# First norm's modulation as two fused VectorE instructions, with another order of the recurrent units and later booked transfer landings

## The chip, the cores and the metric

The kernel runs on one core of one Trainium2 chip. The metric is the device time of one launch in microseconds (us). In this text PE is TensorE, DVE is VectorE, ACT is ScalarE, POOL is GpSimd and SP is the engine that issues most transfers.

## The reference

One inference step of a two-layer decoder trunk: 512 prompt rows of width 1024, and 8 samples of 8 rows each, all in fp32. Layer 0 is a recurrent block (a causal convolution of width 4, sigmoid gates, a linear recurrence, a gelu branch), layer 1 sliding-window attention; each is followed by a gated feed-forward block of inner width 2816. Every norm is modulated by a shift and a scale that a vector of conditions gives, so the first steps are:

```
def rms_norm(x, g):
    y = xf * lax.rsqrt(jnp.mean(xf * xf, axis=-1, keepdims=True) + EPS)
    return (y * g.astype(jnp.float32)).astype(x.dtype)

sh1, sc1, g1, sh2, sc2, g2 = ada_mod(c, ada_w[l], ada_b[l], 6)   # silu(c) @ ada_w + ada_b
h = modulate(rms_norm(x, norm_g[l, 0]), sh1, sc1)                # h * (1 + scale) + shift
xr, yg = jnp.split(h @ w_in, 2, axis=-1)                         # recurrent block
...
x = x + g1[:, None, :] * out
h = modulate(rms_norm(x, norm_g[l, 1]), sh2, sc2)
x = x + g2[:, None, :] * swiglu(h, ffn_w_in[l], ffn_w_out[l])
```

Between the layers one shared projection makes keys and values from the stream. The outputs are the normed stream, the last convolution rows and recurrent states, and the key and value windows.

## The kernel before

**Number format and tiles.** The stream x lies in SBUF with its 1024 features as 8 chunks of 128 partitions and its rows along the free dimension, in two halves A and B of 288 columns (256 prompt columns, HP, and 32 of samples). A product of fp32 accuracy is made from three matmuls in the rounded format fp32r: each operand is split into a high part hi (the value rounded) and a low part lo (the value less hi), and PE adds hi by hi, hi by lo and lo by hi. So one output block of 128 features and one half is 8 chunks x 3 = 24 matmuls of 128x288. Weights come by DMA into four slots `raw`; ACT makes their high part (CAST `wh<-raw`), DVE their low part (TENSOR_TENSOR `wh<-raw,wh`), which also frees the raw slot. Modulated activations are the tiles `h` (one for each half, hi and lo side by side); gates read `ta` (hi) and `tb` (lo).

**The first norm.** `modulated` (line 911 of before) does chunk by chunk x times the inverse root (`rstd`, which the trace calls `acc`), then times scale plus shift (`mods`), then the split. The string M1 names engines: the first product by DVE, but by POOL for chunks 2 and 5; the value v by one DVE TENSOR_SCALAR into a `tb` slot; hi by ACT directly from the first product with scale and bias; lo = v - hi by DVE. The sample columns have their own function. The modulation comes from PE in four groups of two chunks (`ada_first`): PE's columns go to PSUM (`ada`), ACT copies them (`td`), PE transposes them back (`ada<-ident,td`) and DVE adds bias and norm weight (`mods`). The weights of all this, `ada_w` and `rnn_w_in`, come in a fixed order of transfers from SP.

**The order of work.** The kernel's functions do not issue instructions: a recorder collects every operation, which is why all of them carry line 505, and `schedule` (line 240) writes the order for each of the five engines once, with a cost model. Engines then run that order strictly, each instruction waiting for its operands' semaphores. The model's guess when a transfer has landed decides what it sets before what. It keeps one clock for the DMA engines, which starts at OFF (line 70), and books a landing at the end of a transfer's turn plus a margin (line 406):

```
b = max(s + op.cost + 650, dma_free[0])
dma_free[0] = b + op.lat
op.end = b + op.lat + (1700 if op.i >= self.strict else 1000)
```

The first transfers, up to `strict` (line 2029), have the smaller margin. A tile from a pool gets a slot when the schedule finds one free, so the order also decides which transfer waits for whom: 4 `raw` slots, 10 of `wh`, 37 of `sl`, 7 of `ta`, 8 of `tb`, 4 of `td`.

The recurrent block's own sequence is the string RNN (line 59): x0 to x7 are blocks of the convolution branch (16 or 24 matmuls a half), g0 to g7 the gates of a block (matmuls of 128x300 on `ta`, `tb`), y0 to y7 the gelu branch's blocks, which are multiplied by the recurrence's result and split into `sl` tiles. Half B follows half A by some units. ACT holds one table of functions at a time; exp, sqrt, gelu and silu are in separate tables (the gates use tanh, exp and sqrt, the y blocks gelu), and each change is an ACT_TABLE_LOAD.

`x_turn` (line 639) transposes the rows of x through PE at the start, `x_half` (line 1987) sums their squares. PE runs filler matmuls on the identity (`mm<-ident`) while it has no work.

Of the kernel before, what the change touches and what calls it, by code (L numbers as in the profile page):

```python
# [12 lines left out]
F32 = mybir.dt.float32  # L13
# [3 lines left out]
ALU = mybir.AluOpType  # L17
# [38 lines left out]
QUAD = (3, 4, 5, 6)  # L56
QK = 2
YT = lambda td, ta, sl: td
RNN = "x0 x1 x2 x3 x4 x5 g0 g1 g2 y2 y0 y1 g3 g4 x6 y3 x7 g5 y5 g6 y6 g7 y4 y7"
ATT = "q0A q2A a0A q1A q0B a2A q1B q3A a0B q2B q4A a1A a1B a4A a3A q3B a2B q5A q4B a3B q6A a5A q5B q7A a6A a4B s0A a5B s1A s2A s3A q6B q7B a7A s0B s1B a6B fA a7B o0A s2B s3B o1A o2A fB"  # L60
LOOK = {"PE": 24, "DVE": 24, "ACT": 24, "POOL": 24, "SP": 24}
NRAW = 4
# [2 lines left out]
XB = 100  # L65
NFILL = 60
AE = 100
ME = 30
YG = 6
OFF = 2300.0  # L70
AF_ = (1, 2, 4, 4)
NSL, NTA, NTB, NTD = 37, 7, 8, 4

# [70 lines left out]
class Recorder:  # L144
# [95 lines left out]
    def schedule(self):  # L240
# [64 lines left out]
        while n_left:  # L305
# [92 lines left out]
            if op.lat:  # L398

                free[e] = s + op.cost  # L400
                if e == "POOL":
                    op.end = s + op.cost + (3000 if op.i < self.strict else 5000)
                else:
                    b = max(s + op.cost + 650, dma_free[0])
                    dma_free[0] = b + op.lat
                    op.end = b + op.lat + (1700 if op.i >= self.strict else 1000)
            else:
                op.end = free[e] = s + cost
            for n in op.tiles:
# [122 lines left out]
def trunk_kernel(ctx, tc, a):  # L532
# [106 lines left out]
    def x_turn(t):  # L639
        src = xt[t].f  # L640
        if t < 4:
            for q in range(2):
                pt = aux()
                for k in range(4):
                    c = 4 * q + k
                    T.transpose(pt[:, k * P : (k + 1) * P], src[:, c * P : (c + 1) * P], ident[:])
                dst = x[t // 2][:, 4 * q : 4 * q + 4, (t % 2) * P : (t % 2) * P + P]
                (V.tensor_copy, S.copy)[q](dst, pt.rearrange("p (k n) -> p k n", k=4))
        else:
            pt = aux()  # L650
            for c in range(4):
                T.transpose(pt[:, c * P : (c + 1) * P], src[:, c * P : (c + 1) * P], ident[:])
            for h in range(2):
                V.tensor_copy(x[h][:, :, HP:HC].rearrange("p (q c) n -> p q c n", q=2), pt.rearrange("p (c q n) -> p q c n", c=4, q=2)[:, :, :, 32 * h : 32 * h + 32])
        xt[t].done()
# [255 lines left out]
    def modulated(h, gsc, gsh, how, cs=slice(0, KC), xn=None, known=False):  # L911

        batch, se, ne, ve, le = how.split()
        pick = {"V": V, "G": G}
        for c in range(cs.start, cs.stop):
            if (c - cs.start) % int(batch) == 0:
                modulated_samples(h, gsc, gsh, pick[se], slice(c, min(c + int(batch), cs.stop)), xn, known)
            t, u = xn[c] if xn else ta(), tb()
            n, v = t.f[:, 0:HP], u.f[:, 0:HP]
            hi, lo = [h4r(h)[:, c, i, 0:HP] for i in range(2)]  # L920
            if not known:
                pick[ne[c % len(ne)]].tensor_tensor(n, x[h][:, c, 0:HP], rstd[h][:, 0:HP], ALU.mult)
            w = ve[c % len(ve)]
            if w == "S":
                S.activation(v, n, AF.Identity, bias=mp(gsh, c), scale=mp(gsc, c))
            else:
                V.tensor_scalar(v, n, mp(gsc, c), mp(gsh, c), ALU.mult, ALU.add)
            if w == "F":
                S.activation(hi, n, AF.Identity, bias=mp(gsh, c), scale=mp(gsc, c))
            else:  # L930
                S.copy(hi, v)
            pick[le[c % len(le)]].tensor_tensor(lo, v, hi.bitcast(F32), ALU.subtract)
            if not xn or known:
                t.done()
            u.done()
        if known:
            xn[KC].done()
# [85 lines left out]
    def h4r(h):  # L1023
        return H[h].r.rearrange("p (c s n) -> p c s n", c=KC, s=2)
# [962 lines left out]
    def x_half(h):  # L1987
        st = tst[h]
        for t in ((0, 1, 4), (2, 3))[h]:

            r = raws() if h else None
            w = r.f if h else x[1].rearrange("p c n -> p (c n)")[:, D * (t % 2) : D * (t % 2 + 1)]
            n, y = (512, tst[1][:, 2:3]) if t == 4 else (D, st[:, t % 2 : t % 2 + 1])
            src, dst = xt[t].f[:, 0:n], w[:, 0:n]
            if t % 2 == 0:
                S.activation(dst, src, AF.Square, accum_out=y)
            else:
                V.tensor_tensor_reduce(out=dst, in0=src, in1=src, op0=ALU.mult, op1=ALU.add, scale=1.0, scalar=0.0, accum_out=y)
            if h:
                r.done()  # L2000
            if t == 4:
                V.tensor_copy(tst[1][0:64, 5:6], y[64:128])
                V.tensor_tensor(y[0:64], y[0:64], tst[1][0:64, 5:6], ALU.add)
                V.tensor_scalar(tst[0][0:32, 2:3], y[0:32], 1.0 / D, EPS, ALU.mult, ALU.add)
                V.tensor_scalar(tst[1][32:64, 2:3], y[32:64], 1.0 / D, EPS, ALU.mult, ALU.add)
# [49 lines left out]

    stages.append(jobs)
    stages.append(ffn1)
    pace = [0.0]

    def do(j, h):  # L2060
        for u in j.need:
# [121 lines left out]
```

## Time and profile before

| what | before |
|---|---|
| three runs, us | 1246.37, 1246.6, 1246.83 (median 1246.6) |
| profiled execution, us | 1247.9 |
| its span (first to last record), us | 1246.1 |
| PE busy, us | 1232.9 |
| DVE, ACT, POOL busy, us | 897.3, 653.3, 465.4 |
| table loads of ACT | 21 of 1283 ns |

The profiled execution took 1.3 us more than the median of the runs, and 1.8 us of it lie outside its span. In the rows below, times in a timeline are microseconds from the start of the span; the number in brackets is how long the engine stood idle ahead of the row, and what ended that. Groups give busy time, then mean ns of one instruction; a group's mean duration is longer than the distance between two starts, as an engine's instructions overlap a little.

### The profile page before, as it was taken

How to read it: one execution, taken by the hardware profiler on the slowest of the kernel's cores; microseconds unless marked ns; L12 is line 12 of the kernel's file. 1: busy time of each engine (PE TensorE's matmuls, PEld its weight loads, DVE VectorE, ACT ScalarE, POOL GpSimd, SP SyncE). 2: the span in 40 equal slices, each digit the busy share in tenths (PEclk: the TensorE clock that was granted, in tenths of full speed). 3: DMA queues.
4: the chain of work that ended last, by engine and by line, in shares of the span. 5: the costliest groups of instructions: out<-in, count | busy, mean ns of one | idle time of the engine just before them, and what ended most of it. 6: DMA issues, size and time to landing. Idle time of an engine off the chain costs nothing.

```text
span 1246.1 us, 25373 instructions
## 1 busy us (share of the span) xinstructions
PE 1232.9 (99%) x9590; PEld 1171.4 (94%) x9590; DVE 897.3 (72%) x2137; ACT 653.3 (52%) x1461; POOL 465.4 (37%) x645
## 2 busy tenths in 40 slices
PE   8999999999999999999999999999999999999997
PEld 7888989999999999998999988999999999999997
DVE  6998875895674786477578888568767667747766
ACT  5678954852452444145367679448425435525533
POOL 3264540163441452246125445100436246335500
PEclk9999999999999999999999999999999999999999
DMA  9985554326556555445433321422332323323222
GB/s 310 300 274 173 179 167 139 124 76 212 170 189 200 170 171 165 165 142 155 118 90 69 70 61 46 122 71 100 99 103 69 112 76 102 102 85 86 85 86 76
DMA packets 221164, 165.39 MB, mean 133 GB/s; under 512 B 23817, under 2 KB 205993, under 8 KB 221010
## 3 DMA queue, kind: packets, MB, share of 16 engines
q1 hardware_dynamic: 220434, 163.39, 43.1%
q8 instruction: 75, 1.23, 0.4%
q0 software_dynamic: 608, 0.39, 0.1%
q14 instruction: 47, 0.39, 0.1%
HBM read 160.85 MB, written 4.87 MB: 133 GB/s over the span
## 4 chain that ended last, share of the span: by engine, by line
PE 92%; DVE 3%; DMA 2%; ACT 1%; POOL 1%; issue 0%; SPq 0%; DVEq 0%; ACTq 0%
PE mm L505 87%; PE ada L505 5%; DVE sl L505 1%; DVE ta L505 1%; DMA reg<-in_x_prompt_dram 1%; DMA raw<-in_rnn_w_in_dram 1%; DMA wh<-in_ada_w_dram 1%; DVE wh L505 0%; DMA raw<-in_ffn_w_out_dram 0%; POOL td L505 0%; DVE h L505 0%; DVE x L505 0%; ACT wh L505 0%; SPq L505 0%; DVE tb L505 0%
## 5 line engine op out<-in xcount | busy, mean ns | idle before, releaser
L505 PE MATMUL mm<-h,wh 128*128 128x288 f32 x4080 | 584.1, 297 | 0.3
L505 PEld LDWEIGHTS mm<-h,wh 128*128 128x128 f32 x4080 | 553.0, 188 | 12.1 <-issue 6.0
L505 PE MATMUL mm<-sl,wh 128*128 128x288 f32 x3237 | 464.2, 296 | 0.3 <-ACT sl L505 0.3
L505 PEld LDWEIGHTS mm<-sl,wh 128*128 128x128 f32 x3237 | 439.8, 188 | 6.1 <-issue 5.0
L505 ACT CAST wh<-raw 128x512 fp32r<-128x512 f32 (+3 forms) x394 | 270.5, 706 | 304.2 <-PE mm L505 188.2
L505 DVE TENSOR_TENSOR wh<-raw,wh 128x512 fp32r<-128x512 f32 (+3 forms) x396 | 362.1, 935 | 58.4 <-ACT wh L505 53.9
L505 POOL TENSOR_TENSOR raw<-raw 128x512 f32<-128x512 f32 x78 | 115.2, 1477 | 175.5 <-DVE wh L505 157.9
L505 DVE SCALAR_TENSOR_TENSOR x<-mm,mods,x 128x256 f32<-128x256 f32 x160 | 77.3, 483 | 124.6 <-PE mm L505 123.8
L505 POOL TENSOR_TENSOR x<-x,ta 128x32 f32<-128x32 f32 x120 | 41.6, 347 | 241.1 <-DVE ta L505 241.1
L505 POOL TENSOR_TENSOR raw<-raw,raw 128x512 f32<-128x512 f32 x78 | 116.1, 1488 | 4.6
L505 PE MATMUL mm<-tb,wh 128*128 128x288 f32 (+1 forms) x500 | 92.7, 299 | 1.3 <-DVE td L505 1.3
L505 POOL TENSOR_TENSOR td<-td,td 128x288 f32<-128x288 f32 x39 | 33.1, 850 | 135.8 <-ACT td L505 121.3
L505 PEld LDWEIGHTS mm<-tb,wh 128*128 128x128 f32 x500 | 74.5, 188 | 4.3 <-DVE td L505 2.9
L505 ACT ACTIVATE ta<-x 128x288 f32<-128x288 f32 (+1 forms) x56 | 24.4, 442 | 63.4 <-POOL x L505 40.4
L505 PE MATMUL mm<-ta,wh 128*128 128x288 f32 (+1 forms) x259 | 57.4, 297 | 0.0
L505 DVE TENSOR_TENSOR td<-mm,td 128x288 f32<-128x288 f32 x78 | 34.4, 452 | 21.6 <-PE mm L505 21.0
L505 DVE TENSOR_TENSOR sl<-td,sl 128x288 fp32r<-128x288 f32 x65 | 41.2, 637 | 8.9 <-ACT sl L505 8.9
L505 PE MATMUL ada<-reg,cz 128*32 128x512 f32 (+1 forms) x408 | 47.0, 547 | 0.0
L505 PEld LDWEIGHTS mm<-ta,wh 128*128 128x128 f32 x259 | 42.8, 188 | 1.0 <-ACT ta L505 1.0
L505 ACT ACTIVATE td<-td 128x288 f32<-128x288 f32 x39 | 17.3, 443 | 44.2 <-DVE td L505 44.2
L505 ACT ACTIVATE ta<-ta,stat 128x256 f32<-128x256 f32 (+2 forms) x72 | 32.5, 473 | 10.8 <-DVE stat L505 10.4
L505 ACT COPY ta<-mm 128x288 f32<-128x288 f32 (+1 forms) x51 | 19.1, 376 | 36.2 <-PE mm L505 35.1
(221 smaller groups left out, 1243.9 us busy)
## 6 DMA issues: line engine op xcount, KB each, us to landing
raw<-in_ffn_w_in_dram SPq DMA_DIRECT2D x88, 512.0 KB
reg<-in_ada_w_dram SPq DMA_DIRECT2D x72, 512.0 KB
raw<-in_ffn_w_out_dram SPq DMA_DIRECT2D x32, 384.0 KB
raw<-in_ffn_w_out_dram SPq DMA_DIRECT2D x32, 320.0 KB
reg<-in_kv_ada_w_dram SPq DMA_DIRECT2D x14, 512.0 KB
raw<-in_rnn_w_in_dram SPq DMA_DIRECT2D x13, 512.0 KB
wh<-in_ada_w_dram SPq DMA_DIRECT2D x24, 256.0 KB
raw<-in_rnn_w_out_dram SPq DMA_DIRECT2D x8, 512.0 KB
```

The lines of the kernel that those rows point to most:

```text
L505: self.rec.add(eng, lambda: getattr(obj, name)(*map(real, args), **{k: real(v) for k, v in kw.items()}), cost, outs, ins, func, lat, port, ...
```

## The change

In `modulated`, for chunks 2 to 7 (`c >= FU`) where no product is handed in, DVE makes n = (x * scale) * rstd in one SCALAR_TENSOR_TENSOR, ACT makes hi = n + shift rounded, and DVE makes lo = (n + shift) - hi in a second SCALAR_TENSOR_TENSOR. No `tb` slot and no POOL instruction is used for these 256 columns. The first product therefore reads `mods`, which it did not before. The sequence RNN is another one: g0 comes ahead of x5, y1 y2 y0 in place of y2 y0 y1, g5 y5 y3 x7 in place of y3 x7 g5 y5. OFF goes from 2300 to 1800, and the booked margins from 1000 and 1700 to 2000 and 2900. The new constants SQ, XE and A0 have the values that give the same instructions as before.

```diff
-RNN = "x0 x1 x2 x3 x4 x5 g0 g1 g2 y2 y0 y1 g3 g4 x6 y3 x7 g5 y5 g6 y6 g7 y4 y7"
+RNN = "x0 x1 x2 x3 x4 g0 x5 g1 g2 y1 y2 y0 g3 g4 x6 g5 y5 y3 x7 g6 y6 g7 y4 y7"
...
+A0 = 0.0
+FU = 2
+SQ = 3
+XE = "VSVS"
...
-OFF = 2300.0
+OFF = 1800.0
...
-                    op.end = b + op.lat + (1700 if op.i >= self.strict else 1000)
+                    op.end = b + op.lat + (2900 if op.i >= self.strict else 2000)
...
-                (V.tensor_copy, S.copy)[q](dst, pt.rearrange("p (k n) -> p k n", k=4))
+                (V.tensor_copy if XE[t // 2 * 2 + q] == "V" else S.copy)(dst, pt.rearrange("p (k n) -> p k n", k=4))
...
+            hi, lo = [h4r(h)[:, c, i, 0:HP] for i in range(2)]
+            if c >= FU and not xn:
+                t = ta()
+                n = t.f[:, 0:HP]
+                V.scalar_tensor_tensor(n, x[h][:, c, 0:HP], mp(gsc, c), rstd[h][:, 0:HP], ALU.mult, ALU.mult)
+                S.activation(hi, n, AF.Identity, bias=mp(gsh, c))
+                V.scalar_tensor_tensor(lo, n, mp(gsh, c), hi.bitcast(F32), ALU.add, ALU.subtract)
+                t.done()
+                continue
             t, u = xn[c] if xn else ta(), tb()
             n, v = t.f[:, 0:HP], u.f[:, 0:HP]
-            hi, lo = [h4r(h)[:, c, i, 0:HP] for i in range(2)]
...
-            if t % 2 == 0:
+            if t % 2 == 0 or t > SQ:
...
-    pace = [0.0]
+    pace = [A0]
```

The first place in the program is on DVE, the last group of the first norm (chunks 6 and 7; `h_485` is half B before, `h_483` after). Before, the rows from the group's modulation on are these:

```order
L505 SCALAR_TENSOR_TENSOR mods<-ada_835,abT,vecT 128x9 x2
L505 TENSOR_TENSOR mods<-ada_835,abT 128x18
L505 TENSOR_TENSOR tb_850<-ta_664,mods 128x64
L505 TENSOR_SCALAR tb_854<-ta_775,mods 128x256
L505 TENSOR_TENSOR tb_850<-tb_850,mods 128x64
L505 TENSOR_SCALAR tb_862<-ta_811,mods 128x256
L505 TENSOR_TENSOR tb_866<-ta_813,mods 128x64
L505 TENSOR_SCALAR tb_870<-ta_815,mods 128x256
L505 TENSOR_TENSOR h_328<-tb_850,h_328 128x2x32
L505 TENSOR_TENSOR h_328<-tb_854,h_328 128x256
L505 TENSOR_TENSOR h_328<-tb_862,h_328 128x256
L505 TENSOR_TENSOR tb_866<-tb_866,mods 128x64
```

After, the rows from the same modulation on are these:

```order
L509 SCALAR_TENSOR_TENSOR mods<-ada_823,abT,vecT 128x9 x2
L509 TENSOR_TENSOR mods<-ada_823,abT 128x18
L509 SCALAR_TENSOR_TENSOR ta_839<-x_64,mods,acc_69 128x256
L509 TENSOR_TENSOR tb_846<-ta_428,mods 128x64
L509 SCALAR_TENSOR_TENSOR ta_849<-x_64,mods,acc_69 128x256
L509 TENSOR_TENSOR tb_846<-tb_846,mods 128x64
L509 TENSOR_TENSOR tb_858<-ta_653,mods 128x64
L509 SCALAR_TENSOR_TENSOR h_330<-ta_839,mods,h_330 128x256
L509 TENSOR_TENSOR tb_858<-tb_858,mods 128x64
L509 SCALAR_TENSOR_TENSOR h_330<-ta_849,mods,h_330 128x256
L509 TENSOR_TENSOR h_330<-tb_846,h_330 128x2x32
L509 TENSOR_TENSOR h_483<-tb_858,h_483 128x2x32
```

The four first products of the group, which stood ahead of the modulation before (among them `ta_775`, `ta_811`), now stand behind it and read `mods`; two of them, and two low parts, follow the rows shown, with one weight's low part between.

The second place is on PE, where gate g0's first matmuls stand (`h_485` and `h_483` are half B; the gates read `ta` and `tb`). Before, they stand behind a block of half A:

```order
L505 MATMUL mm_1102<-h_328,wh_1027 128x288
L505 MATMUL mm_1139<-ta_973,wh_1001 128x300
L505 MATMUL mm_1139<-ta_973,wh_1088 128x300
L505 MATMUL mm_1139<-tb_1111,wh_1001 128x300
L505 MATMUL mm_1147<-ta_973,wh_1001 128x300
L505 MATMUL mm_1147<-ta_973,wh_1088 128x300
L505 MATMUL mm_1147<-tb_1111,wh_1001 128x300
L505 MATMUL mm_1154<-h_485,wh_833 128x288 x2
```

After, they stand behind a block of half B:

```order
L509 MATMUL mm_1054<-h_483,wh_672 128x288
L509 MATMUL mm_1108<-ta_990,wh_965 128x300
L509 MATMUL mm_1108<-ta_990,wh_1082 128x300
L509 MATMUL mm_1113<-ta_990,wh_965 128x300
L509 MATMUL mm_1113<-ta_990,wh_1082 128x300
L509 MATMUL mm_1116<-h_483,wh_820 128x288 x2
L509 MATMUL mm_1116<-h_483,wh_894 128x288
L509 MATMUL mm_1116<-h_483,wh_820 128x288
L509 MATMUL mm_1125<-h_330,wh_1110 128x288 x2
L509 MATMUL mm_1116<-h_483,wh_820 128x288
L509 MATMUL mm_1116<-h_483,wh_894 128x288
L509 MATMUL mm_1116<-h_483,wh_820 128x288 x2
```

Before, all six of the two gate products stand together behind 18 matmuls of the next block; now the four that read `ta` come first, right behind the block of 24, then ten matmuls of two other blocks, then the two that read `tb`.

The third place is on DVE, where the first unit of the feed-forward block's output weights is split (`wh` of 128x640 from `raw`; `td` holds silu of the gate, which this DVE instruction multiplies by the other half's product before it is split for PE). Before, the rows from the end of the input weights' splits on are these:

```order
L505 TENSOR_TENSOR wh_3960<-raw_3841,wh_3960 128x512
L505 TENSOR_TENSOR wh_4000<-raw_3778,wh_4000 128x512
L505 TENSOR_TENSOR wh_4029<-raw_3849,wh_3911 128x640
L505 TENSOR_TENSOR sl_4038<-td_3827,sl_4016 128x288
L505 TENSOR_TENSOR wh_4045<-raw_3857,wh_3926 128x640
L505 TENSOR_TENSOR sl_4055<-ta_3758,sl_3992 128x288
L505 TENSOR_TENSOR mm_4003<-mm_4003,ta_3938 128x288
L505 COPY td_4062<-mm_4003 128x288
L505 TENSOR_TENSOR td_4062<-mm_3984,td_4062 128x288
L505 TENSOR_TENSOR wh_4091<-raw_4023,wh_4078 128x640
L505 TENSOR_TENSOR td_4008<-mm_4003,td_4008 128x288
L505 TENSOR_TENSOR wh_4112<-raw_4032,wh_4095 128x640
```

After, the rows from the same splits on are these:

```order
L509 TENSOR_TENSOR wh_3960<-raw_3819,wh_3960 128x512
L509 TENSOR_TENSOR wh_3981<-raw_3756,wh_3981 128x512
L509 TENSOR_TENSOR wh_4005<-raw_3756,wh_4005 128x512
L509 TENSOR_TENSOR wh_4027<-raw_3835,wh_3921 128x640
L509 TENSOR_TENSOR sl_4036<-td_3805,sl_4022 128x288
L509 TENSOR_TENSOR sl_4043<-ta_3736,sl_3971 128x288
L509 TENSOR_TENSOR wh_4050<-raw_3929,wh_3994 128x640
L509 TENSOR_TENSOR mm_3996<-mm_3996,ta_3917 128x288
L509 COPY td_4062<-mm_3996 128x288
L509 TENSOR_TENSOR wh_4075<-raw_3990,wh_4058 128x640
L509 TENSOR_TENSOR td_4062<-mm_3962,td_4062 128x288
L509 TENSOR_TENSOR td_3988<-mm_3996,td_3988 128x288
```

Before, the split of the third load (`raw_4023`) stands between the two `td` rows that precede PE's products; after, the first load's split is already over (row `wh_3914<-raw_3827`, six rows ahead of those shown), and the splits of the third and the fourth (`raw_3929`, `raw_3990`) both stand ahead of both `td` rows.

## The prediction

> **What bounds the kernel now.** I read the page first, then the waits of TensorE (PE), then the windows of the first 180 us, then the places where PE stands still. The page:
>
> ```profile
> span 1246.1 us, 25373 instructions
> PE 1232.9 (99%) x9590; PEld 1171.4 (94%) x9590; DVE 897.3 (72%) x2137; ACT 653.3 (52%) x1461; POOL 465.4 (37%) x645
> PE 92%; DVE 3%; DMA 2%; ACT 1%; POOL 1%; issue 0%; SPq 0%; DVEq 0%; ACTq 0%
> ```
>
> PE is busy 1232.9 of 1246.1 us and makes up 92% of the chain that ended last. The change touches no matmul of the model, so it can only move what PE waits for. Those waits, by kind (us in total, times, longest):
>
> ```profile
> PE mm L505 <- DVE td L505: 1.3, 1, 1.3
> PE ada L505 <- ACT td L505: 1.0, 1, 1.0
> PE mm L505 <- ACT sl L505: 0.3, 1, 0.3
> ```
>
> Seen whole, there is little to win: 1.3 us on a VectorE (DVE) result, 1.0 on a ScalarE (ACT) result, 0.3 on another; the rest are waits of the very start and two of 0.2. Windows (first PE, PEld, DVE, ACT, POOL busy, then granted clock, DMA share, GB/s):
>
> ```profile
> 30.00:40.00 10.00, 8.96 (x113) 7.88 (x112) 8.29 (x30) 6.49 (x15) 1.11 (x2) 1.00 1.10 336
> 60.00:80.00 20.00, 20.00 (x153) 17.81 (x146) 17.56 (x41) 13.13 (x26) 13.42 (x38) 1.00 0.95 296
> 80.00:100.00 20.00, 19.98 (x151) 18.30 (x150) 17.47 (x31) 17.08 (x34) 10.29 (x23) 1.00 0.59 190
> 100.00:120.00 20.00, 20.00 (x154) 16.80 (x153) 16.16 (x33) 17.08 (x29) 8.35 (x19) 1.00 0.46 140
> 120.00:140.00 20.00, 20.00 (x150) 19.82 (x149) 18.45 (x34) 17.90 (x37) 10.56 (x18) 1.00 0.73 238
> 140.00:160.00 20.00, 20.00 (x154) 16.78 (x153) 17.76 (x32) 18.54 (x34) 13.00 (x30) 1.00 0.53 166
> ```
>
> Up to 40 us the sixteen DMA engines have no room (share 1.10): the first norm runs inside a stage that loads set. From 60 to 160 us, the recurrent block, PE is full, but ACT is busy 83.73 of 100 us (13.13 + 17.08 + 17.08 + 17.90 + 18.54) and DVE 87.40: that stage has the least spare room beside PE. The base of my sum is the profiled execution (1247.9 us, its span 1246.1); it lies 1.3 above the median of the runs, 1246.6, to which I apply the difference.
>
> **The change part by part.** *First norm, chunks 2 to 7, both halves: 12 chunk-halves.* Groups of DVE and of GpSimd (POOL) in the norm's stretch, busy us and mean ns:
>
> ```profile
> L505 DVE SCALAR_TENSOR_TENSOR sl<-td,vecT,sl 128x300 f32<-128x300 f32 x18 | 8.3, 518 | 0.0
> L505 DVE TENSOR_TENSOR h<-tb,h 128x256 fp32r<-128x256 f32 x16 | 6.6, 420 | 0.0
> L505 DVE TENSOR_SCALAR tb<-ta,mods 128x256 f32<-128x256 f32 x14 | 5.7, 407 | 0.0
> L505 DVE TENSOR_TENSOR ta<-x,acc 128x256 f32<-128x256 f32 x10 | 4.1, 417 | 0.0
> L505 POOL TENSOR_TENSOR ta<-x,acc 128x256 f32<-128x256 f32 x4 | 3.5, 875 | 16.8 <-ACT acc L505 10.5 <-DVE ta L505 5.4 <-DVE tb L505 0.9
> ```
>
> Before, a chunk-half costs DVE 417 + 407 + 420 = 1244 ns, or 827 where POOL makes the first product (chunks 2 and 5, four chunk-halves). After, it costs two SCALAR_TENSOR_TENSOR of 128x256. That form with this shape is not in the trace: the floor is the TENSOR_TENSOR of the same shape, 417, the ceiling the 128x300 form, 518; I take 470, nearer the middle since 300 columns are 17% more. So 8 x (940 - 1244) = -2.4 us and 4 x (940 - 827) = +0.5: DVE is relieved of 1.9 us (3.3 to 0.6 at the ends: 8 x -0.41 to -0.21, 4 x +0.01 to +0.21), POOL of 4 x 0.875 = 3.5. POOL is idle most of that time, and DVE's relief is worth something only where PE waits for DVE.
>
> The Trainium skill, Vector Engine (DVE) Microarchitecture Reference, section 7 (points that are easy to get wrong), says the contrary of a cheap fusion: a scalar-tensor-tensor with two SBUF sources that are not bf16 runs at half throughput. The 128x300 row above has just such sources and takes 518 ns, near the plain two-source rows; the trace does not show the halving. By the rule the two instructions would take longer than the three; that is a rival below.
>
> But the order matters more than the sum: before, the product x times root needed no modulation and filled DVE's idle time ahead of it; now it needs the scale, so it comes after. The last group, chunks 6 and 7 (DVE, then PE):
>
> ```profile
> 43.85 1.22 DVE L505 TENSOR_TENSOR ta<-x,acc 128x256 f32<-128x256 f32 x4
> 46.87 0.36 DVE L505 SCALAR_TENSOR_TENSOR mods<-ada,abT,vecT 128x9 f32<-128x9 f32 x2 [0.91 <-PE ada L505]
> 50.50 0.55 DVE L505 TENSOR_TENSOR h<-tb,h 128x64 fp32r<-128x64 f32 x2
> 50.97 0.95 DVE L505 TENSOR_TENSOR wh<-raw,wh 128x768 fp32r<-128x768 f32 x1
> ```
>
> ```profile
> 46.50 0.33 PE L505 MATMUL ada<-ident,td 128*128 128x128 f32 x1
> 46.59 12.21 PE L505 MATMUL mm<-h,wh 128*128 128x288 f32 x88
> ```
>
> Before, four products ran at 43.85, ahead of the modulation at 46.87, and the last piece of half B was there at 51.05. By the new order DVE does eight scalar-tensor-tensors and the small ones between 47.3 and the end, with the split of one weight (0.95) ahead of the last two: 8 x 0.40 (starts of such instructions in a row stand about 0.07 closer than their mean) + 8 small at 0.16 + 0.95 = 5.4, so 52.7 at worst and, as the last two are half B's last two chunks, chunk 6 at about 52.0. PE takes 12.21 / 88 = 0.139 per matmul; 37 of them stand ahead of chunk 6 of half B, so it is asked for at 46.59 + 5.1 = 51.7. That is a new wait of 0.3 us; bounds 0 and 1.0. **+0.3.**
>
> *Start.* In the new order PE transposes the bias vector before the eight of x, and it has one filler more.
>
> ```profile
> 5.45 1.04 PE L505 MATMUL mm<-ident,reg 128*128 128x128 f32 x8
> 7.17 0.23 PE L505 MATMUL mm<-ident,sl 16*128 16x16 f32 x1 [0.68 <-DMA sl<-in_ada_b_dram]
> ```
>
> The eight began at 5.45; after, they follow the vector's transposition, which ends at 7.40, so they begin 1.9 later, of which the wait of 0.68, now ahead of them, is given back. Behind them stands this pinch:
>
> ```profile
> 36.62 1.04 ACT L505 CAST wh<-raw 128x1024 fp32r<-128x1024 f32 x1 [2.77 <-DMA raw<-in_rnn_w_in_dram]
> 37.58 0.26 ACT L505 COPY td<-ada 128x128 f32<-128x128 f32 x1
> 37.89 0.33 PE L505 MATMUL ada<-ident,td 128*128 128x128 f32 x1 [1.04 <-ACT td L505]
> ```
>
> ACT copies what PE needs only behind a cast that waits for a weight until 36.62. The order of ACT there, and of the loads up to that weight, is the same after, so the pinch stays and swallows lateness up to 1.04 us ahead of it. **0** (0 to +1.2, which is 1.9 less 0.7, if that cover were gone).
>
> *Units' order, the booked start of the transfers, later booked landings.* They move the recurrent block's instructions. Gate g0 follows the 24 matmuls of one unit directly. Before:
>
> ```profile
> 60.58 5.88 PE L505 MATMUL mm<-h,wh 128*128 128x288 f32 x42
> 59.26 1.28 ACT L505 ACT_TABLE_LOAD   x1
> 64.27 0.47 DVE L505 TENSOR_TENSOR tb<-sl,ta 128x300 fp32r<-128x300 f32 x1
> 66.57 0.30 PE L505 MATMUL mm<-tb,wh 128*128 128x300 f32 x1
> ```
>
> Its low part is ready at 64.74 and used at 66.57; after, g0 stands behind the first 24 of the 42 matmuls, so it starts at 60.58 + 24 x 0.139 = 63.9, and the low part is asked for 14 matmuls later, at 65.85: of 1.8 us slack 1.1 stays, and the lateness of the norm's end (0.3 to 1.7) lies against it. I take +0.1, bounds 0 and 0.6. ACT's table loads go from 21 to 23, both extra ones in this stage: 2 x 1.28 = 2.6 us on an engine with 100 - 83.73 = 16.3 idle. Hidden on average; I charge +0.1 for places where they are not, bounds 0 and 2.6. **+0.2.**
>
> *End of the block.* PE's 0.3 wait:
>
> ```profile
> 174.35 0.43 ACT L505 CAST sl<-td 128x288 fp32r<-128x288 f32 x1 [0.93 <-DVE ta L505]
> 174.83 5.40 PE L505 MATMUL mm<-sl,wh 128*128 128x288 f32 x38 [0.25 <-ACT sl L505]
> ```
>
> The new order has one table load fewer in this tail and the last gate unit's matmuls earlier: **-0.3** (0 to -0.4).
>
> *First feed-forward block, at 284 us*, PE's longest wait (DMA from the chain, then ACT, DVE, PE):
>
> ```profile
> 278.74 5.09 DMA raw<-in_ffn_w_out_dram
> ```
>
> ```profile
> 275.90 3.72 DVE L505 TENSOR_TENSOR wh<-raw,wh 128x512 fp32r<-128x512 f32 x4
> 284.67 0.82 DVE L505 TENSOR_TENSOR wh<-raw,wh 128x640 fp32r<-128x640 f32 x1 [2.15 <-ACT wh L505]
> 285.41 0.45 DVE L505 TENSOR_TENSOR td<-mm,td 128x288 f32<-128x288 f32 x1
> ```
>
> ```profile
> 283.91 0.73 ACT L505 CAST wh<-raw 128x640 fp32r<-128x640 f32 x1 [3.22 <-DMA raw<-in_ffn_w_out_dram]
> 285.92 0.67 PE L505 MATMUL mm<-tb,wh 128*128 128x288 f32 x3 [1.27 <-DVE td L505]
> ```
>
> The third load of the out weights waits until a slot is freed by the third of the four splits (275.90 + 3 x 0.93 = 278.69); DVE's td stands behind that load's split. After, the first out weight is split ahead of the group, so the third load goes early; the fourth takes the slot, freed by the second split, one split (3.72 / 4 = 0.93) sooner. It lands at 278.74 - 0.93 + 5.09 = 282.9; cast 0.73, split 0.8, and now both td behind it, 0.4 each: 285.2 against 285.9, so the wait falls from 1.3 to 0.6. **-0.7** (-1.3 if it lands in time, +1.0 if the load goes no sooner and both td queue behind it).
>
> The rest, from 300 us on, is nearly the same order; 0, give or take 0.5. Sum: 0.3 + 0 + 0.2 - 0.3 - 0.7 = **-0.5**: 1247.4 for an execution like the profiled one, 1246.1 by the median.
>
> **The rivals.** *A, slower: the recurrent block becomes ACT's.* The two table loads (2.6) and the norm's late end (up to 1.7) fall where gates come sooner, and ACT, at 18.54 of 20 from 140 to 160, cannot give it back. PE then waits 4.3, less the 1.0 above: 1246.6 + 3.3 = 1249.9. It decides once g0's low part is over 1.1 us late and ACT's idle time from 60 to 160 falls under some 3 us. Against: 16.3 us idle now.
>
> *B, faster: every wait behind the start goes.* 1.04 at 37.9, 1.27 at 285.9, 0.25 at 174.8: -2.6, 1244.0, and somewhat less if the start shrinks with them. For: DVE and POOL are lighter up to 50 us. Against: the wait at 37.9 ends with a landing that the order of loads sets.
>
> *C, the fused form at half rate.* If the form with both sources in SBUF ran so, a 128x256 would take some 0.82 us, twice the plain 0.41. Eight of them in the last group end 8 x (0.82 - 0.47) = 2.8 later, and the wait at 51.7 grows by as much: 1246.1 + 2.8 = 1248.9. Against it: the 518 itself, a quarter over the plain form of 256. The rule for it is the one of the Trainium skill cited above.
>
> *D, nothing of it reaches PE*, as the stalls only swap places: 1246.6.
>
> **How the numbers follow.** A measurement of this kernel tells 0.2%, 2.5 us, from no change. The forecast's own sum has 0.53, D 0.11, both within 2.5 us; C 0.05, within too; A 0.16, over 1249.1; B 0.15, under 1244.1. Faster 0.15, same 0.69, slower 0.16. The range takes in the bounds of the terms and half of A and B: 1243.7 to 1249.3.
>
> **What would show it.** Right: DVE scalar-tensor-tensors of 128x256 at 0.42 to 0.52; PE's wait at 37.9 unchanged near 1.0; a wait near 51.7 under 1; none at 174.8; one near 285 of about half; 23 table loads, ACT near 86 busy from 60 to 160. Wrong: PE waits of over 1 us between 60 and 160, a pinch that moved, or a wait of over 2 us on the out weights.

## The result, and the profile after

| | before | after |
|---|---|---|
| median of 20 runs each, us | 1246.65 (1245.9 to 1247.34) | 1244.22 (1243.24 to 1245.89) |
| ratio, 95% interval | 1 | 0.9982 [0.9976, 0.9988] |
| span of the profiled execution, us | 1246.1 | 1242.9 |

The change makes the kernel 2.4 us faster. The forecast was 1246.1, that is 0.5 faster; the range held the time. Most of the gain lies where the forecast had most of its own, at 285 us, at twice the forecast size and in part by another step than the one told. The two profiled executions differ by 3.2 us, 0.8 more than the medians. The page of after:

```profile
span 1242.9 us, 25366 instructions
PE 1231.9 (99%) x9592; PEld 1170.8 (94%) x9592; DVE 889.1 (72%) x2129; ACT 655.7 (53%) x1463; POOL 461.7 (37%) x641
PE 93%; DVE 2%; DMA 2%; ACT 1%; POOL 1%; issue 0%; SPq 0%; DVEq 0%; ACTq 0%; POOLq 0%
```

DVE is 8.2 us lighter and POOL 3.7, yet PE's share of the chain is the same within one per cent: most of that relief lay beside PE's work. What PE waits for after (all of 0.2 us and more):

```profile
PE mm L509 <- POOL few L590: 1.4, 1, 1.4
PE mm L509 <- DMA reg<-in_x_prompt_dram: 1.3, 1, 1.3
PE mm L509 <- ACT sl L509: 0.3, 1, 0.3
PE mm L509 <- DMA sl<-in_ada_b_dram: 0.3, 1, 0.3
PE ada L509 <- DMA wh<-in_ada_w_dram: 0.2, 1, 0.2
```

The wait of 1.3 on DVE (at 285.9) and that of 1.0 on ACT (at 37.9) are gone. At the start a wait for a transfer of x grew to 1.3, from two of at most 0.4. The windows of two stages, first before, then after (PE, PEld, DVE, ACT, POOL busy, then granted clock, DMA share, GB/s):

```profile
60.00:160.00 100.00, 99.98 (x753) 89.52 (x746) 87.40 (x169) 83.73 (x158) 55.62 (x127) 1.00 0.65 206
250.00:300.00 50.00, 48.73 (x368) 46.10 (x367) 39.52 (x66) 21.92 (x42) 23.68 (x21) 1.00 0.55 168
```

```profile
60.00:160.00 100.00, 99.85 (x749) 91.24 (x746) 86.71 (x172) 86.07 (x161) 49.73 (x104) 1.00 0.64 199
250.00:300.00 50.00, 50.00 (x380) 47.60 (x379) 40.89 (x68) 21.90 (x42) 24.13 (x22) 1.00 0.56 170
```

Most of the gain stands in the second row: PE idles 1.27 us between 250 and 300 us before, and not at all after. In the recurrent block (first row) PE was full and still is; ACT's busy time rose by 2.3 us, and no wait came of it.

More than busy time tells PE's lateness: the start of a weight matmul in one trace less the start of the same matmul in the trace of before, at places where both have the same work behind them. For after it is -0.4 when PE leaves the start (16 `ada` matmuls stand at 58.38, before at 58.73), 0.1 behind the first gates (the next 16 at 70.53, before at 70.44), 0.0 at 115, -0.1 at 175 and at 280, and falls by 1.56 at 285. Behind that it falls in three steps of 0.3, at 441, 466 and 831 us, and by some 0.5 spread over the rest, to -3.1. The three steps appear as well in kernels whose order there is the one of before (runs 3, 4 and 5 below), so I take them as delays of the one profiled execution of before, which lies 1.3 us above its median, and not as a part of the change. They make 0.9 us, about the 0.8 by which the spans differ more than the medians.

At 285 us, PE before, then PE after:

```profile
281.68 0.56 PE L505 MATMUL mm<-sl,wh 128*128 128x288 f32 x3
282.08 0.99 PE L505 MATMUL mm<-tb,wh 128*128 128x288 f32 x6
282.91 1.73 PE L505 MATMUL mm<-sl,wh 128*128 128x288 f32 x12
```

```profile
278.61 0.83 PE L509 MATMUL mm<-sl,wh 128*128 128x288 f32 x5
...
282.20 1.35 PE L509 MATMUL mm<-sl,wh 128*128 128x288 f32 x9
283.39 0.96 PE L509 MATMUL mm<-tb,wh 128*128 128x288 f32 x6
284.19 1.75 PE L509 MATMUL mm<-sl,wh 128*128 128x288 f32 x12
285.78 0.58 PE L509 MATMUL mm<-tb,wh 128*128 128x288 f32 x3
```

The last row, three matmuls on `tb`, has no bracket: what it reads is ready when PE asks. Before, PE asked for it at 284.65 (285.92 less the wait of 1.27). It asks later in after because more work stands ahead: 14 matmuls on `sl` (5 and 9) where before has 3, while the matmuls on `h`, `ta` and `tb` up to that row are as many as before. The 11 more follow behind the three in before, as part of a long row on `sl`; by their place I take them for the first products with the out weights, which the trace does not name. At 0.133 us each they make 1.5 us, and fill the wait.

ACT after, then DVE, then SP's issues of the third and the fourth load:

```profile
280.80 0.73 ACT L509 CAST wh<-raw 128x640 fp32r<-128x640 f32 x1 [0.81 <-DVE wh L509]
```

```profile
283.06 0.81 DVE L509 TENSOR_TENSOR wh<-raw,wh 128x640 fp32r<-128x640 f32 x1
283.80 0.45 DVE L509 TENSOR_TENSOR td<-mm,td 128x288 f32<-128x288 f32 x1
285.18 0.46 DVE L509 TENSOR_TENSOR td<-mm,td 128x288 f32<-128x288 f32 x1 [0.93 <-PE mm L509]
```

```profile
272.31 5.29 SPq L509 DMA_DIRECT2D raw<-in_ffn_w_out_dram  x2
```

ACT's cast of the fourth load (280.80) waits for DVE to release a weight slot and not for the landing. SP's row holds two issues, the third load's at 272.31 and the fourth's, which starts at 277.23; so the fourth landed within 280.80 - 277.23 = 3.6 us, where the row of before, the third load's, had 5.09. DVE ends the split of the fourth load at 283.87. The second `td` is over at 285.64, 0.2 sooner than in before (285.86), and what it waited for, 0.93 us long, is a product of PE and not a load.

### The profile page after: what moved, and what is told of

It is laid out like the page before. It is cut to its first block, busy times and chain, and to the rows that moved or that the text cites. A ratio compares the mean times of both kernels' runs of the same rounds, so it can differ in the third digit from the quotient of the medians.

```text
span 1242.9 us, 25366 instructions
## 1 busy us (share of the span) xinstructions
PE 1231.9 (99%) x9592; PEld 1170.8 (94%) x9592; DVE 889.1 (72%) x2129; ACT 655.7 (53%) x1463; POOL 461.7 (37%) x641
## 4 chain that ended last, share of the span: by engine, by line
PE 93%; DVE 2%; DMA 2%; ACT 1%; POOL 1%; issue 0%; SPq 0%; DVEq 0%; ACTq 0%; POOLq 0%
PE mm L509 88%; PE ada L509 5%; DMA reg<-in_x_prompt_dram 1%; DMA raw<-in_rnn_w_in_dram 1%; DVE sl L509 1%; POOL sl L509 1%; DVE wh L509 0%; DMA wh<-in_ada_w_dram 0%; DVE h L509 0%; DVE tb L509 0%; DVE ta L509 0%; SPq L509 0%; ACT wh L509 0%; ACT L509 0%; ACT sl L509 0%
## 5 line engine op out<-in xcount | busy, mean ns | idle before, releaser
L509 ACT CAST sl<-td 128x288 fp32r<-128x288 f32 x65 | 28.0, 432 | 25.0 <-POOL td L509 15.9
```

Of the source, the lines that this page charges most:

```text
L509: self.rec.add(eng, lambda: getattr(obj, name)(*map(real, args), **{k: real(v) for k, v in kw.items()}), cost, outs, ins, func, lat, port, ...
```

## The experiments

Each was timed in five rounds against before on its own chip; "L" stands for the later booked landings, "F" for the fused norm, "R" for the new sequence of units, "O" for OFF at 1800. The first theory was that the landings alone bring the whole gain, by the order that they give to the feed-forward block, at 270 to 285 us above all. The rivals were that the fused norm or the new sequence brings part of it, or that each helps only with the others.

| run | parts | median, us | ratio to before, 95% interval |
|---|---|---|---|
| after | F R O L | 1244.22 | 0.9982 [0.9976, 0.9988] |
| 1 | L | 1243.82 | 0.9979 [0.9970, 0.9987] |
| 2 | F | 1249.31 | 1.0024 [1.0015, 1.0033] |
| 3 | R | 1254.5 | 1.0061 [1.0048, 1.0074] |
| 4 | F R O | 1251.74 | 1.0044 [1.0030, 1.0057] |
| 5 | L from 200 to 300 us only | 1245.84 | 0.9992 [0.9983, 1.0001] |
| 6 | L from 300 us on only | 1245.98 | 0.9994 [0.9985, 1.0003] |
| 7 | R O L | 1254.3 | 1.0061 [1.0048, 1.0075] |
| 8 | F L | 1248.51 | 1.0014 [1.0005, 1.0023] |
| 9 | R O L, three instructions moved | 1252.31 | 1.0043 [1.0029, 1.0057] |
| 10 | F R L | 1244.58 | 0.9983 [0.9974, 0.9993] |
| 11 | L with margins of 2500 and 3500 | 1245.56 | 0.9992 [0.9983, 1.0001] |
| 12 | L O | 1243.51 | 0.9973 [0.9962, 0.9983] |

**Run 1, the landings alone.**

```diff
-op.end = b + op.lat + (1700 if op.i >= self.strict else 1000)
+op.end = b + op.lat + (2900 if op.i >= self.strict else 2000)
```

> The kernel before with the later booked landings alone (+2000 and +2900); old norm, old units' order, old start of transfers. Theory 1, the landings make the gain by the order they give in the feed-forward blocks: 2.0 to 2.8 us faster than before (ratio 0.9977 to 0.9984), PE's wait of 1.3 us at 285 gone, the two of 0.2 to 0.3 near 441 and 466 gone. Theory 2, the fused norm makes it by relieving DVE: within 0.6 us of before. Theory 3, the units' order makes it: within 0.6 us of before.

Measured 2.6 us faster. PE's waits:

```profile
PE mm L509 <- POOL few L590: 1.4, 1, 1.4
PE mm L509 <- DMA reg<-in_x_prompt_dram: 1.0, 1, 1.0
PE mm L509 <- DMA sl<-in_ada_b_dram: 0.3, 1, 0.3
PE mm L509 <- DVE few L509: 0.2, 1, 0.2
```

The waits of before at 37.9, 174.8 and 285.9 are all gone with one edit. (The first is no gain of the edit: runs 3 and 6, whose order at the start is that of before, have 0.6 and 0.4 there in place of 1.0.) PE's lateness falls by 1.55 at 285 us and by 0.26 at 175, as there is no wait of 0.25 on `sl` any more. The first theory holds: this is the whole gain of after; the 0.4 us more is not told apart by the two intervals.

**Run 2, the fused norm alone.**

```diff
+FU = 2
...
+if c >= FU and not xn:
```

> The kernel before with the fused norm alone. Theory 1: within 0.8 us of before, the wait at 285 still 1.2 to 1.5 us, since the third load of the output weights stands where it stood. Theory 2: 1.8 to 2.6 us faster. Theory 3: within 0.8 us of before.

Measured 2.8 us slower, which none of the three theories had. PE between 141 and 151 us:

```profile
145.06 0.54 PE L509 MATMUL mm<-tb,wh 128*128 128x300 f32 x2 [1.55 <-DVE tb L509]
146.06 4.19 PE L509 MATMUL mm<-h,wh 128*128 128x288 f32 x18 [0.46 <-ACT ta L509]
```

A gate's operands are late, a hundred microseconds behind the norm that was edited. Two waits of 2.0 us in all, and the 18 matmuls behind them take 0.23 us each, against 0.133: the clock was down for 3.4 us (last section), which costs another 1.7. The wait at 285 stays (1.3). The cheaper form does not reach PE; what it does is move the schedule's choices in the block behind it.

**Run 3, the new sequence alone.**

```diff
-RNN = "x0 x1 x2 x3 x4 x5 g0 g1 g2 y2 y0 y1 g3 g4 x6 y3 x7 g5 y5 g6 y6 g7 y4 y7"
+RNN = "x0 x1 x2 x3 x4 g0 x5 g1 g2 y1 y2 y0 g3 g4 x6 g5 y5 y3 x7 g6 y6 g7 y4 y7"
```

> The kernel before with the new units' order alone. Theory 1: within 0.8 us of before, the wait at 285 still 1.2 to 1.5 us. Theory 2: the same as theory 1. Theory 3: 1.8 to 2.6 us faster.

Measured 8.0 us slower, which no theory had either. Two waits in the recurrent block (PE):

```profile
91.09 4.72 PE L509 MATMUL mm<-h,wh 128*128 128x288 f32 x22 [2.43 <-DVE wh L509]
128.91 0.87 PE L509 MATMUL mm<-ta,wh 128*128 128x300 f32 x2 [3.52 <-ACT td L509]
```

The 22 matmuls of the first row take 4.72 us, 0.21 each, against 0.139: the clock was down (last section). The expectation also had the wait at 285 stay, and it is gone, though the order of every engine from 180 us on is that of before. PE comes there 9.1 us later than in before; the third load is issued 8.6 us later (287.29) and cast 6.8 later (290.72), so it landed within 3.4 us in place of 5.1. Why it landed faster the run does not show. A wait that vanishes so, in a kernel that is late elsewhere, is no gain.

**Run 4, everything but the landings.**

```diff
-op.end = b + op.lat + (2900 if op.i >= self.strict else 2000)
+op.end = b + op.lat + (1700 if op.i >= self.strict else 1000)
```

(against after)

> The changed kernel with the old booked landings (+1000 and +1700); fused norm, new units' order and earlier start of transfers stay. Theory 1: within 0.8 us of before, so 1.6 to 3.2 us slower than the changed kernel, the wait at 285 back at 1.2 to 1.5 us. Theories 2 and 3: 1.8 to 2.6 us faster than before, as the changed kernel.

Measured 5.3 us slower than before. The same two places, PE:

```profile
90.45 3.20 PE L509 MATMUL mm<-h,wh 128*128 128x288 f32 x22 [1.43 <-DVE wh L509]
126.65 0.55 PE L509 MATMUL mm<-ta,wh 128*128 128x300 f32 x2 [3.54 <-ACT td L509]
```

Fused norm and sequence together do not free each other; it takes the landings too. The expectation had the time of before and the wait at 285 back at 1.2 to 1.5; it missed both, and that wait is gone as in run 3, with the order of before there and a third load that landed within 3.3 us. That the sequence and the fused norm bring a part of the gain is out.

**Runs 5 and 6: where do the landings act?** The later margins hold only for transfers that the model starts between 200 and 300 us (run 5), or from 300 us on (run 6, `if s >= 300000`). Run 5's line:

```diff
-op.end = b + op.lat + (1700 if op.i >= self.strict else 1000)
+op.end = b + op.lat + ((2900 if op.i >= self.strict else 2000) if 200000 <= s < 300000 else (1700 if op.i >= self.strict else 1000))
```

> The kernel before with the later booked landings only where the scheduler's own clock is between 200 and 300 us; all else as before. Theory 1a, the wait on the output weights at 285 us is most of the gain: 1.2 to 1.7 us faster than before, that wait gone, the waits of 0.2 near 441, 466 and 831 still there. Rival 1b, the gain is spread over the start and the later blocks and the wait at 285 only moves: within 0.6 us of before.

> The kernel before with the later booked landings only from 300 us of the scheduler's clock on. Theory 1a: 0.5 to 1.1 us faster than before, the wait at 285 as before (1.3), the three of 0.2 behind it gone. Rival 1b: 1.5 us faster or more.

Run 5 has the fall at 285 us (1.53) but lost 1.2 us at the start, whose instructions are those of before. PE there, and its window:

```profile
19.12 1.85 PE L509 MATMUL mm<-ident,reg 128*128 128x128 f32 x8 [1.94 <-DMA reg<-in_x_prompt_dram]
```

```profile
20.00:24.00 4.00, 4.00 (x25) 3.98 (x24) 3.31 (x8) 1.62 (x5) 1.60 (x3) 0.67 1.11 339
```

In that execution the transfer of x came 1.9 us after it was asked for, and PE then ran at a clock of 0.67. In before and in runs 3 and 6 the longest such wait was 0.4 to 0.5. So 1.0 us in the median, with an interval that reaches 1.0001, neither confirms nor denies by itself; the trace does. Its order on PE, DVE and ACT is that of before up to 269 us and again from 290 us on, so what lies between is all that the edit changed, and there PE's lateness falls by 1.53. The expectation that the small steps at 441, 466 and 831 us need the landings missed: they are gone in run 5 too, where the order behind 300 us is old. That is what shows them to be delays of the one execution. In run 6 PE still waits at 285 us:

```profile
285.10 0.66 PE L509 MATMUL mm<-tb,wh 128*128 128x288 f32 x3 [1.02 <-DVE td L509]
```

and its lateness shows no step behind it beyond those three; its 0.9 us in the median has an interval that reaches 1.0003, so it is not told from nothing. The 11 matmuls on `sl` stand ahead of the three on `tb` in every run with the later landings between 200 and 300 us (12 in run 11), and in none without. The landings act at 270 to 285 us, and by some tenths up to 175.

**Run 7, without the fused norm.**

```diff
-FU = 2
+FU = 8
```

(against after)

> The changed kernel with the old norm: new units' order, earlier start of transfers and later landings stay. If the fused norm gives nothing of its own once landings are booked later: within 0.8 us of the changed kernel, so 1.6 to 3.2 us faster than before. If it pays by relieving DVE in the recurrent block: 1 us or more slower than the changed kernel, by new waits between 60 and 160 us.

Measured 7.5 us slower than before, 10.1 slower than after: the second branch of the expectation, with its new waits between 60 and 160 us. PE, then ACT and DVE at the weight that PE waits for:

```profile
91.48 4.70 PE L509 MATMUL mm<-h,wh 128*128 128x288 f32 x22 [2.44 <-DVE wh L509]
```

```profile
85.62 1.03 ACT L509 CAST wh<-raw 128x1024 fp32r<-128x1024 f32 x1
```

```profile
90.21 1.21 DVE L509 TENSOR_TENSOR wh<-raw,wh 128x1024 fp32r<-128x1024 f32 x1
```

ACT has the high part ready at 86.65; DVE makes the low part only at 90.21, behind instructions of the gates. The schedule's model starts that split at 85.8 us of its own clock, so DVE on the chip runs 4.4 us behind the model there. In after the same split stands at 87.79, and PE does not wait. The sequence therefore costs nothing only together with the fused norm, and (run 4) only with the landings.

**Run 8, landings and fused norm, old sequence.**

```diff
-RNN = "x0 x1 x2 x3 x4 g0 x5 g1 g2 y1 y2 y0 g3 g4 x6 g5 y5 y3 x7 g6 y6 g7 y4 y7"
+RNN = "x0 x1 x2 x3 x4 x5 g0 g1 g2 y2 y0 y1 g3 g4 x6 y3 x7 g5 y5 g6 y6 g7 y4 y7"
```

(against after, with OFF 2300)

> The kernel before with the later landings and the fused norm, old units' order. If the fused norm gives nothing of its own: within 0.8 us of the landings alone, 1.8 to 3.4 us faster than before. If it relieves DVE where PE waits: 3.4 us faster or more. If the fused norm costs what it cost alone (2.8 us): within 0.8 us of before.

Measured 1.7 us slower than before, which none of the three branches had. The waits of run 2 are back, at 145.44 and 146.44 us (1.56 on `tb`, 0.46 on `ta`). After does not have them: beside the landings, the new sequence takes away the waits that the fused norm brings, and the fused norm (run 7) those that the sequence brings.

**Run 9: is the order of a few instructions the cause of run 7's waits?** A further theory: both waits stand behind single instructions that the model set too late or too early. Run 7's kernel, with three instructions moved in the finished order: the late split went five places ahead on DVE, and near 123 us a weight's cast on ACT and its split on DVE went behind the gates' instructions.

```diff
+moved = {1019: 83170.0, 1519: 125153.0, 1520: 126200.0}
+for o in out:
+    o.start = moved.get(o.i, o.start)
+out.sort(key=lambda o: (o.start, o.i))
```

> The kernel of run 7 (new units' order and later landings, old norm: 1254.3 us) with three instructions moved in the finished order, all else and all slots the same: on DVE the split of the weight that PE waits for at 91 us goes six rows up, ahead of the scans; on ACT the cast that stands 3.8 us waiting for a weight slot at 123 us goes behind the gelu evacuations that PE waits for at 129 us, and its split on DVE behind that. Theory 4, PE's two waits come from where those instructions stand in their queues: both waits fall under 0.8 us each, 5 to 9.5 us faster than run 7 (1244.8 to 1249.3). Rival 4b, DVE and ACT have too little capacity there without the fused norm, whatever the order: the waits stay or move by a few us, at most 2 us faster than run 7.

Measured 2.0 us faster than run 7, less than the 5 to 9.5 of the theory and the most that rival 4b allowed. PE, then ACT:

```profile
94.20 0.41 PE L512 MATMUL mm<-tb,wh 128*128 128x300 f32 x1 [0.56 <-DVE tb L512]
...
128.66 0.87 PE L512 MATMUL mm<-ta,wh 128*128 128x300 f32 x2 [3.52 <-ACT td L512]
```

```profile
123.69 0.64 ACT L512 ACTIVATE sl<-td,vecT 128x300 f32<-128x300 f32 x1 [4.92 <-DVE td L512]
```

At the first place the theory holds: 2.44 became three waits of 0.6 and less (1.1 in all). At the second it falls: with the cast out of the way, ACT's next instruction waits 4.92 us for DVE, and PE's 3.52 stays to the digit. DVE itself is late there. What makes it late, over the stretch from 90 to 120 us, was not settled; rival 4b, too little capacity on DVE and ACT without the fused norm, is not out.

**Run 10, the booked start of the transfers back.**

```diff
-OFF = 1800.0
+OFF = 2300.0
```

(against after)

> The changed kernel with the transfers' booked start back at 2300. If that part gives nothing of its own: within 0.8 us of the changed kernel, 1.6 to 3.2 us faster than before. If the set of parts only fits together by chance, a wait of 1.5 us or more comes up between 60 and 180 us: 2 us or more slower than the changed kernel.

0.9983 against 0.9982: OFF brings nothing that these runs can tell.

**Run 11, margins of 2500 and 3500.**

```diff
-op.end = b + op.lat + (1700 if op.i >= self.strict else 1000)
+op.end = b + op.lat + (3500 if op.i >= self.strict else 2500)
```

> The kernel before with landings booked later still (+2500 and +3500), all else as before. If the gain is that loads are booked near where they land, more margin gives no more: within 0.8 us of the landings alone at +2000 and +2900, 1.8 to 3.4 us faster than before. If it grows with the margin: 3.4 us faster or more. If the margin only happens to fit: slower than before.

The fall at 285 us is there (1.56), and is given back at the start, PE and its window:

```profile
7.39 0.23 PE L509 MATMUL mm<-ident,sl 16*128 16x16 f32 x1 [1.78 <-DMA sl<-in_ada_b_dram]
```

```profile
8.00:12.00 4.00, 4.00 (x24) 3.65 (x24) 2.38 (x7) 1.21 (x3) 0.00 (x0) 0.57 1.10 340
```

PE comes out of the start 1.36 us later than before. This wait is one that varies (between none of note and 1.8 over the runs), so the run does not show that a larger margin is worse; it shows that it gains nothing more at 285 us. The median, 1.4 us under before, misses the 1.8 to 3.4 that was expected.

**Run 12, the best of both: landings and OFF, old norm, old sequence.**

```diff
-OFF = 2300.0
+OFF = 1800.0
-op.end = b + op.lat + (1700 if op.i >= self.strict else 1000)
+op.end = b + op.lat + (2900 if op.i >= self.strict else 2000)
```

> The kernel before with the later landings (+2000 and +2900) and the earlier start of transfers (1800), old norm, old units' order: the candidate for a better version. If the start gives nothing: within 0.8 us of the landings alone, 1.8 to 3.4 us faster than before. If it helps the first 20 us: 3.4 us faster or more.

The lowest median of all, 3.4 us under before and 0.7 under after; its interval overlaps those of after and of run 1. As far as the intervals tell, a kernel with none of the norm's and the sequence's edits is as fast as the whole change.

## Why the prediction was right in sign and half right in size

**At 285 us, the term that was mis-sized.** "The wait falls from 1.3 to 0.6", -0.7; measured: it falls to nothing, and PE's lateness falls by 1.56, the wait of 1.27 and 0.3 around it. The steps on the loads were right as told: the first out weight is split ahead of the group, the third load goes early, the fourth takes a slot one split sooner, both `td` stand behind it. The step that failed is one that the sum took for granted: that PE asks when it asked before. The forecast had both `td` made at 285.2, with PE asking at 284.65. In after the second `td` is made only at 285.64, and yet PE does not wait, as it asks at 285.78, behind 11 matmuls more. So the earlier load is not what took the wait away: it made the operand 0.2 us sooner, and the 11 matmuls filled the rest. The bound that I gave, "-1.3 if it lands in time", was reached for another reason.

The landing was off too, but did not decide: I took the 5.09 us of before's third load for the fourth. It is issued at 277.23, 0.6 us sooner than I had it, and lands within 3.6. With the landing that I forecast, 282.9, its cast and split would still have been over by 284.4, ahead of the `td` at 285.18 that waited for PE. The 5.09 is no constant of the transfer: before, four loads are issued in a row there (SP), and after, the fourth goes alone.

```profile
278.74 2.38 SPq L505 DMA_DIRECT2D raw<-in_ffn_w_out_dram  x4
```

The company is not all of it, for runs 3 and 4 issue the same four in a row and the third lands within 3.4 and 3.3 us; the rest stays open.

**The start.** Forecast zero; PE leaves the start 0.4 us earlier, and not by the change. PE before, then PE, ACT and PE after:

```profile
33.73 1.95 PE L505 MATMUL ada<-reg,cz 128*32 128x128 f32 x64
```

```profile
19.06 1.06 PE L509 MATMUL mm<-ident,reg 128*128 128x128 f32 x8 [1.32 <-DMA reg<-in_x_prompt_dram]
...
34.57 1.95 PE L509 MATMUL ada<-reg,cz 128*32 128x128 f32 x64
```

```profile
36.23 1.05 ACT L509 CAST wh<-raw 128x1024 fp32r<-128x1024 f32 x1 [1.74 <-DMA raw<-in_rnn_w_in_dram]
```

```profile
37.49 0.33 PE L509 MATMUL ada<-ident,td 128*128 128x128 f32 x1
```

The wait for x grew, and PE is 0.84 us later than before at 34.57; behind ACT's cast, which still waits for a weight, it goes on at 37.49, against 37.89. So the pinch did swallow the lateness, as told, and nothing of its wait is left. The sign that I named for it, a wait "unchanged near 1.0", was a wrong one: a wait that swallows lateness shrinks by it. So was its counterpart among the signs of being wrong, "a pinch that moved". The 0.4 is the landing of that weight, 0.39 earlier; run 6, whose order there is that of before, leaves the start 0.5 earlier as well, so this lies in the one execution of before. Over the runs the waits at the start vary by more than the change moves them, so this term could not have been forecast to better than about 1 us.

**The end of the norm, +0.3 at 51.7.** No wait came; zero. The lower bound of the term. The price of the new form was right (DVE, groups between 19 and 62 us):

```profile
L509 DVE SCALAR_TENSOR_TENSOR h<-ta,mods,h 128x256 fp32r<-128x256 f32 x12 | 5.7, 481 | 0.1
L509 DVE SCALAR_TENSOR_TENSOR ta<-x,mods,acc 128x256 f32<-128x256 f32 x12 | 5.7, 478 | 0.0
```

478 and 481 ns against 470 forecast. Rival C, the half rate, would have shown 820: it is out, and so is the rule of the Trainium skill behind it (Vector Engine (DVE) Microarchitecture Reference, section 7) for this form, shape and pair of SBUF sources. A nearer row than the two I used was on the page of before: the same form at 128x256, 160 times, at 483 ns (`x<-mm,mods,x`, one source in PSUM). And the ends of DVE's relief come to 3.2 and 0.8 by the ends of the price, not to 3.3 and 0.6.

**The gates and table loads, +0.2.** The gap ahead of g0's last two matmuls is only 0.15 us, but between 58 and 70 us PE falls from 0.35 ahead of before to 0.09 behind: +0.4, within the bounds. 23 table loads and 86.07 us of ACT from 60 to 160 came as told, and stay hidden in after.

**The tail of the block, -0.3.** The wait of 0.25 at 174.8 went, and one of 0.34 came at 165.9; PE's lateness falls by 0.1 there. About zero.

**The rest, 0 give or take 0.5.** Some 0.5 spread over 900 us, apart from the three delays of before's own execution.

Sum of what was measured, from the start to the rest and the three delays: -0.4 + 0 + 0.4 - 0.1 - 1.56 - 0.5 - 0.9 = -3.1, as PE's lateness at the end. The 0.9 and the 0.4 of the start are the 1.3 us by which the profiled execution of before lies above its median; that of after lies 0.4 above its own. That leaves 3.1 - 1.3 + 0.4 = 2.2, against 2.4 in the medians.

**The rivals.** B (every wait behind the start goes, 1244.0) came closest in time, in part by luck: it counted the whole 1.04 at 37.9 as gain, and there the reason against it held, since PE went on only behind a landing and came out 0.4 us earlier by that landing alone. A (the recurrent block becomes ACT's) is not what after does, but runs 2, 3, 4, 7 and 8 show that block tip over in five of the builds with only some of the parts, at up to 8 us, and run 9 in a sixth. It is not ACT's busy time that decides it: run 3 keeps ACT busy for 651.9 us, less than before's 653.3, and its waits name DVE's split of a weight and a copy that ACT makes late. The prediction treated the parts as terms that add up, and gave the sequence and the norm a cost of tenths each. Alone they cost 8.0 and 2.8 us; only the set as a whole, or none of the two, costs nothing there. The prediction has no reason why this set fits there and its parts do not; that the whole set was what was run was its luck.

## What to carry to other kernels

Where a planner sets the order of an engine's instructions, the guess of when transfers land can be worth more than the instructions: here the two margins alone gained what the whole change did. Take a bundled change apart and time its parts alone and in pairs: here one part carried the gain, and two others only cancelled each other's harm, and that only with the first in place. When an order changes, work out anew when the waiting engine asks, and not only when its operand comes: other work set ahead of a wait fills it. And do not carry a landing time from the trace of before into a stage whose loads have been moved.

## What the runs showed of the hardware that I had not expected

A wait of PE costs more than its length when the granted clock falls behind it. In every trace here a stretch of half clock ahead of the last 10 us lasts 3.41 us, and it starts a whole number of 3.41 us behind the first full clock of the execution. Run 3 cut at these borders, around its wait of 2.43 us:

```profile
87.84:91.26 3.42, 0.99 (x9) 0.74 (x6) 3.42 (x6) 3.40 (x9) 3.17 (x5) 1.00 0.90 266
91.26:94.67 3.41, 3.41 (x15) 3.41 (x16) 3.41 (x6) 1.05 (x3) 3.41 (x9) 0.50 0.99 326
```

The clock is 0.50 for one stretch, and a matmul takes 0.24 us in place of 0.133. The wait of 2.43 cost PE about 4.1 us and that of 3.52 about 5.2: the wait, and half of the time at half clock. The same followed the two waits of 2.0 in all (run 2) and those of 1.94 (run 5) and 1.78 (run 11). But behind the wait of 3.54 in run 4 the clock is whole:

```profile
121.48:124.89 3.41, 1.64 (x15) 0.56 (x7) 3.28 (x7) 1.87 (x5) 3.22 (x8) 1.00 0.75 232
124.89:128.30 3.41, 1.65 (x12) 1.65 (x13) 3.41 (x7) 3.39 (x7) 3.33 (x8) 1.00 0.93 332
128.30:131.72 3.42, 3.42 (x27) 3.42 (x26) 3.42 (x6) 2.63 (x7) 3.40 (x6) 1.00 0.75 242
```

This wait lies across a border, with 1.77 us idle in one stretch and 1.76 in the next. So what counts is how long PE idles within one stretch, not how long the wait is. In all the traces between 15 us and the last 10 us of the span, the nine stretches with 1.93 us idle or more were followed by half clock, and all those with 1.77 or less by full clock. In the first 10 us, where PE's matmuls are small, this does not hold: 0.86 us idle (run 4) was followed by half clock, 1.13 (before) by full clock.

The Trainium skill, TensorE: Matmul & The Clock Gate, Part 1 (the HAM clock gate), says that the clock halves after an idle window of about 3.4 us, and that the window runs freely and does not start anew with a kernel. The half clock and the length of 3.41 us agree with run 3, and so do borders that a wait can straddle; that the whole window must be idle does not agree, as 1.93 us of 3.41 were enough.
